# The last stage of a layer kernel: written order for its end, four gate pieces moved into it, other engines for its rows

## The chip, the cores and the metric

The kernel runs on one core of a Trainium2 chip. The metric is the time of one execution on the device in microseconds; lower is better. The core has TensorE (PE, with PEld for its weight loads), VectorE (DVE), ScalarE (ACT), GpSimd (POOL) and SyncE (SP, which issues the DMAs).

## What is computed

One decoder layer on 256 tokens of width 2048, in float32: attention, a mixture of 32 experts of which each token uses two, and an embedding of the layer behind a sigmoid gate; then the final norm.

```python
h = h + mixed @ w_out[i]
m = rms_norm(h, g_moe[i])
h = h + hier_moe(m, ..., w_gate[i], w_up[i], w_down[i])
n = rms_norm(h, g_ple[i])
h = h + jax.nn.sigmoid(n @ w_ple_gate[i]) * (p[i] @ w_ple[i])
return rms_norm(h, g_final)
```

## The kernel before, in words

The tokens are two tiles of 128 rows (`t`), and the 2048 columns are handled in blocks (`BLOCKS`; the last two are 256 wide). The text is about the last stage: while the experts' down products for the later column blocks are still made, the gate product `n @ w_ple_gate` is already summed over the input columns that are finished.

A **unit** of the last two column blocks handles two groups of four experts. `down_rows` makes 32 products into `dn` (L782) and weighs them into `y` on ACT (L790) and DVE (L791); `add_rows` brings them to token rows (L1178) and adds them to `acc` on DVE (L1183). The rows of one unit are added behind the next unit's down products.

A **gate piece** is one 128-row slice of the gate weights by 512 columns. `split_w` cuts it into a high part on ACT and a low part on DVE (L269, L270), two pieces ahead of use, and `gate_part` makes three products for each token tile (L1017 to L1019). There are 56 such pieces, taken from the generator `gate` by `take(steps, n)`, as many for each unit as `PACE` says. Where the last piece of 512 output columns is done, a DVE instruction adds the sum of earlier blocks in PSUM (L1084).

The final 256 input columns come at the very end. Their weights are cut into eight pieces by `last_cuts` (L1041 on ACT; L1042 on DVE, or on POOL for pieces 0, 5 and 6), called **cuts 0 to 7** here. `last_operand` transposes the rows (L1126) and makes `n_hi` on ACT (L1130) and `n_lo` on DVE (L1133). Each of eight **output blocks** (0 to 3 for token tile 0, 4 to 7 for tile 1; 512 columns each) then gets its last two pieces: blocks 0 and 4 need cuts 0 and 1, blocks 3 and 7 need cuts 6 and 7.

For four of the eight blocks, `bank` copies the sum so far into a PSUM bank with ACT (L1145), after a product that sets the bank's state (L1144), and the last products add to it. Then comes `finish`: sigmoid on ACT (L1102), multiplication by the embedding (L1104; blocks 0 to 4 on DVE, 5 to 7 on POOL), addition to `acc` on DVE (L1106), square on ACT with a sum per row (L1108). `norm_rows` makes the factor `r` of a token tile from its four sums (L1091 and L1092 on DVE, a power on POOL, L1093), and `finish_rows` scales each row block by `r` and `g_final` in one DVE instruction (L1119) and issues its output (L1120, on SP's queue). One sigmoid buffer with four places is shared by both token tiles.

What sets the order: the loop over the column blocks stands inside `with tc.manual_schedule():`, which has every engine issue its instructions in the order in which they are written. The part behind that loop, from `last.look(CUT[2])` on, stands outside it; there a scheduler orders each engine's queue, with `RUSH` as a hint of priority for token tile 1. A first sigmoid on a constant (L1149), which makes ACT load the sigmoid's table, also stands outside.

Of the kernel before, what the change touches and what calls it, by code (L numbers as in the profile page):

```python
# [10 lines left out]
F32 = mybir.dt.float32  # L11
# [9 lines left out]
P = 128  # L21
# [15 lines left out]
PLE = 256  # L37
EPS = 1e-6
BIG = 1.0e30
RUSH = ((0, 0, 0, 0, 0), (20, 20, 40, 20, 20))  # L40
CUT = (2, 4, 7, 8)
LAST = (1, 1)
UNITS = (((0, 1), (2, 3), (4, 5), (6, 7)), ((2, 3), (6, 7), (0, 1), (4, 5)))
W4 = 1
ON_V = (0, 1, 2, 3, 4)

EMB = (4, 5)
CUT_G = (0, 5, 6)
LOOK = 2
HURRY = 40  # L50
SECOND = (0, 1)


BLOCKS = ((0, 512), (512, 512), (1024, 512), (1536, 256), (1792, 256))
# [3 lines left out]
PLAN = ((0, (0, 1)), (1, (0, 1)), (2, (0, 1)), (3, (1, 0)))  # L58
WARM = (1, 1)
START = (6, 8)  # L60
PACE = ((0,) + (2,) * 7, (0,) + (2,) * 7, (2, 4, 4, 4), (4, 3, 1, 0))
QA, KA, VA, QB, KB = 0, 1024, 2048, 3072, 4096


# [27 lines left out]
def layer(ctx, tc, T, out):  # L92
# [582 lines left out]
    def take(steps, n):  # L675
        for _ in zip(range(n), steps):
            pass
# [98 lines left out]
        V.tensor_reduce(wrow[:, g : g + 1], tp[:, 0:S], AX.X, ALU.add)  # L776
        V.tensor_scalar(held[:, g, :], tp[:, 0:S], 0.0, None, ALU.is_gt)

    def products(dn, g, wd, q0=0):
        for c in range(2):  # L780
            for q in range(4):
                PE.matmul(  # L782
                    dn[32 * q : 32 * q + 32, :], hid_all[:, g, c, 32 * q : 32 * q + 32], wd[c][:, q0 + q, :],
                    start=(c == 0), stop=(c == 1),
                )

    def weighted(g, dn, y):
# [233 lines left out]
    def cols(cb):  # L1021
        return slice(cb * 512, (cb + 1) * 512)
# [66 lines left out]
    def factor(dst, ss):  # L1089

        V.tensor_reduce(dst, ss, AX.X, ALU.add)  # L1091
        V.tensor_scalar(dst, dst, 1.0 / D, EPS, ALU.mult, ALU.add)  # L1092
        G.tensor_tensor(dst, dst, mhalf, ALU.pow)  # L1093

    def finish(t, cb, ps):
        i = 4 * t + cb
        sg = sgs[:, 512 * (i % 4) : 512 * (i % 4) + 512]
        eb = emb[cb // 2][:, t, 512 * (cb % 2) : 512 * (cb % 2) + 512]
        a = acc[cb][:, t, :]
        E = V if i in ON_V else G  # L1100
        with tc.high_priority(RUSH[t][0]):
            A.activation(sg, ps, AF.Sigmoid, scale=rstd2[:, t : t + 1])  # L1102
        with tc.high_priority(RUSH[t][1]):
            E.tensor_tensor(sg, sg, eb, ALU.mult)  # L1104
        with tc.high_priority(RUSH[t][2]):
            V.tensor_tensor(a, a, sg, ALU.add)  # L1106
        with tc.high_priority(RUSH[t][3]):
            A.activation(sg, a, AF.Square, accum_out=ss4[:, t, cb : cb + 1])  # L1108

    def norm_rows(t):  # L1110
        r = fin.tile([P, 1], F32, name="r", tag="r", bufs=2)
        with tc.high_priority(RUSH[t][4]):
            factor(r, ss4[:, t, :])
        for cb in range(4):
            finish_rows(t, cb, r)

    def finish_rows(t, cb, r):
        o = z[:, t, cols(cb)]
        V.scalar_tensor_tensor(o, acc[cb][:, t, :], r, gfin[:, cols(cb)], ALU.mult, ALU.mult)  # L1119
        nc.sync.dma_start(out[t * P : (t + 1) * P, cols(cb)], o)  # L1120

    def last_operand(t, tp):

# [15 lines left out]

    def bank(t, cb, tag):  # L1140

        ps = psk.tile([P, 512], F32, name="ps", tag=tag, bufs=2 if tag == "sc" else 1)

        PE.matmul(ps, n_hi[0][0:1, 0, 0:P], n_hi[0][0:1, 0:2, :].rearrange("p c t -> p (c t)"), start=True, stop=True)  # L1144
        A.copy(ps, z[:, t, cols(cb)])  # L1145
        return ps


    A.activation(rstd2[:, 0:1], eps, AF.Sigmoid)  # L1149
    mhalf = brt[:, NC + n_groups : NC + n_groups + 1]  # L1150
    G.memset(mhalf, -0.5)
    held_ps = {}
# [1 line left out]
    def down_rows(gs, b, wd, tags, y):  # L1154

        n = BLOCKS[b][1]
        parts = [(j, g, slice(n * j, n * j + n)) for j, g in enumerate(gs)]
        for j, g, part in parts:
            if j < len(tags):
                dn = psk.tile([P, 512], F32, name="dn", tag=tags[j], bufs=1 + (tags[j] == "sc"))  # L1160
            products(dn[:, part], g, wd, 4 * j)
            if len(tags) > 1:
                weighted(g, dn[:, part], y[:, :, part])
        if len(tags) == 1:
            for _, g, part in parts:
                weighted(g, dn[:, part], y[:, :, part])

    def add_rows(gs, b, y):
        n = BLOCKS[b][1]
        ab = block(b)  # L1170
        for t in range(0, NT, 512 // n):
            sc = psk.tile([P, 512], F32, name="sc", tag="sc", bufs=2)
            for i in range(512 // n):
                o = sc[:, n * i : n * i + n]
                rows = slice((t + i) * P, (t + i + 1) * P)
                for j, g in enumerate(gs):
                    for k in range(2):
                        PE.matmul(  # L1178
                            o, held[:, g, rows], y[:, k, n * j : n * j + n],
                            start=(j + k == 0), stop=(j == len(gs) - 1 and k == 1), skip_group_check=True,  # L1180
                        )
            a = ab[:, t : t + 512 // n, :]
            V.tensor_tensor(a, a, sc.rearrange("p (t n) -> p t n", n=n), ALU.add)  # L1183

    with tc.manual_schedule():
# [3 lines left out]
        for b in range(EARLY, len(BLOCKS)):  # L1189
            op = operand(b - 1)  # L1190
            units = [(g,) for g in range(n_groups)] if b < 3 else UNITS[b - 3]
            for u, gs in enumerate(units):
# [7 lines left out]
                if final:  # L1200
                    w_last += [load_gate(b, 0, i)[0] for i in range(W4, 2)]

                    gfin = ring.tile([P, D], "gfin", keep=True)
                    nc.sync.dma_start(gfin, T["g_final"].unsqueeze(0).to_broadcast([P, D]))
                    sgs = ring.tile([P, D], "sg", keep=True)
                    last.look(CUT[0])
                    take(steps, 99)
                    add_rows(*late)
                    banks = {(0, 2): bank(0, 2, "dn")}
                    last.look(CUT[1])  # L1210
                    down_rows(gs, b, wd, ("tp", "sc"), y)
                    add_rows(gs, b, y)
                    break
                down_rows(gs, b, wd, (("tp", "dn")[(len(units) - 1 - u) % 2],), y)
                if late:
# [2 lines left out]
                if u == 0:  # L1218
                    for _ in range(2):
                        take(op, 1)  # L1220
                        take(steps, b > EARLY)
                take(steps, PACE[b - EARLY][u])
                if u == 1:
                    squares(b - 1)
    last.look(CUT[2])

    tp = psk.tile([P, NT, 2, P], F32, name="tpn", tag="tp")
    banks[0, 3] = bank(0, 3, "sc")
    last_operand(0, tp)
    banks[1, 2] = bank(1, 2, "sc")  # L1230
    last.look(CUT[3])
    for t in range(NT):
        for cb in range(4):
            if t == 0:
                last.look(min(8, 2 * cb + LOOK))
            if (t, cb) == SECOND:
                last_operand(1, tp)
            if (t, cb) == LAST:
                banks[1, 3] = bank(1, 3, "tp")
            ps = held_ps[cb][:, t, :] if cb < 2 else banks[t, cb]  # L1240
            for k in range(2):
                gate_part(ps, t, 14 + k, last.ready[2 * cb + k], False, k == 1)
            finish(t, cb, ps)
        norm_rows(t)


NAMES = (
# [41 lines left out]
```

## Time and profile before

| | us |
|---|---|
| median of 3 runs | 900.22 (899.55 to 900.97) |
| the profiled execution | 898.98 |
| its span, first to last instruction | 897.3 |
| PE busy | 818.9 (91%) |
| DVE, ACT, POOL busy | 407.7, 303.7, 73.6 |

A row of a timeline gives start, duration, engine, line, operation, what is written and what is read, and in brackets how long the engine was idle before it and who released it; "x2" merges neighbours of one kind. Times count from the span's start.

### The profile page before, as it was taken

How to read it: one execution, taken by the hardware profiler on the slowest of the kernel's cores; microseconds unless marked ns; L12 is line 12 of the kernel's file. 1: busy time of each engine (PE TensorE's matmuls, PEld its weight loads, DVE VectorE, ACT ScalarE, POOL GpSimd, SP SyncE). 2: the span in 40 equal slices, each digit the busy share in tenths (PEclk: the TensorE clock that was granted, in tenths of full speed). 3: DMA queues.
4: the chain of work that ended last, by engine and by line, in shares of the span. 5: the costliest groups of instructions: out<-in, count | busy, mean ns of one | idle time of the engine just before them, and what ended most of it. 6: DMA issues, size and time to landing. Idle time of an engine off the chain costs nothing. (4 is left out here: it accounts for less than half of the span.)

```text
span 897.3 us, 14941 instructions
## 1 busy us (share of the span) xinstructions
PE 818.9 (91%) x6058; PEld 611.6 (68%) x6058; DVE 407.7 (45%) x857; ACT 303.7 (34%) x624; POOL 73.6 (8%) x93
## 2 busy tenths in 40 slices
PE   9999999999999999999899999998756899989993
PEld 8998987899788886577566656655522455557662
DVE  5778667655565554321212111111200554656666
ACT  5657555644464444100000001010010344334364
POOL 3055133300000001000000000000100000000022
PEclk9999999999999999999999989999978999999997
DMA  9972534445598576499999999999979999999902
GB/s 322 372 214 95 168 115 141 141 142 188 202 415 325 182 278 232 157 415 418 418 420 419 418 418 420 418 419 420 419 304 422 419 420 420 419 420 420 411 5 94
DMA packets 47642, 279.52 MB, mean 312 GB/s; under 512 B 9488, under 2 KB 9808, under 8 KB 16464
## 3 DMA queue, kind: packets, MB, share of 16 engines
q1 hardware_dynamic: 46720, 278.45, 78.2%
q8 instruction: 49, 0.80, 0.4%
q0 software_dynamic: 320, 0.05, 0.2%
q14 instruction: 25, 0.20, 0.1%
q10 hardware_dynamic: 528, 0.01, 0.0%
HBM read 276.39 MB, written 2.10 MB: 310 GB/s over the span
## 5 line engine op out<-in xcount | busy, mean ns | idle before, releaser
L270 DVE TENSOR_TENSOR wl<-w,wh 128x512 fp32r<-128x512 f32 (+1 forms) x208 | 140.4, 682 | 107.1 <-ACT wh L269 102.6
L269 ACT ACTIVATE wh<-w 128x512 fp32r<-128x512 f32 (+1 forms) x208 | 127.1, 615 | 121.1 <-PE ps L289 56.2
L288 PE MATMUL ps<-xn_hi,wh 128*128 128x256 f32 x416 | 118.5, 285 | 0.0
L290 PE MATMUL ps<-xn_hi,wl 128*128 128x256 f32 x416 | 117.9, 283 | 0.2 <-DVE wl L270 0.2
L289 PE MATMUL ps<-xn_lo,wh 128*128 128x256 f32 x416 | 117.7, 283 | 0.0
L694 PE MATMUL px<-gr,h 128*128 128x128 f32 x448 | 105.8, 394 | 10.3 <-DVE gr L684 10.3
L694 PEld LDWEIGHTS px<-gr,h 128*128 128x128 f32 x448 | 100.2, 310 | 21.6 <-DVE gr L684 11.4
L695 DVE TENSOR_TENSOR xg<-px,gmoe 128x512 f32<-128x512 f32 x28 | 19.4, 692 | 142.4 <-PE px L694 142.4
L751 PE MATMUL gu<-wu,xg 128*32 128x256 f32 x1008 | 69.1, 411 | 13.3 <-DMA wu<-in_w_up_dram 11.4
L288 PEld LDWEIGHTS ps<-xn_hi,wh 128*128 128x128 f32 x416 | 78.5, 189 | 1.6 <-issue 1.5
L290 PEld LDWEIGHTS ps<-xn_hi,wl 128*128 128x128 f32 x416 | 78.4, 188 | 1.5 <-issue 0.9
L289 PEld LDWEIGHTS ps<-xn_lo,wh 128*128 128x128 f32 x416 | 78.4, 189 | 0.4 <-issue 0.3
L751 PE MATMUL gu<-wg,xg 128*32 128x256 f32 x1024 | 63.8, 401 | 7.9 <-DVEq L945 6.6
L782 PE MATMUL dn<-wd,hid_all 128*32 128x512 f32 (+1 forms) x640 | 62.6, 513 | 8.2 <-ACT hid_all L763 4.2
L751 PEld LDWEIGHTS gu<-wu,xg 128*32 128x32 f32 x1008 | 34.6, 118 | 43.6 <-DMA wu<-in_w_up_dram 14.3
L791 DVE SCALAR_TENSOR_TENSOR y<-dn,brt,y 128x512 fp32r<-128x512 f32 (+1 forms) x40 | 25.7, 644 | 82.6 <-ACT y L790 82.6
L757 ACT ACTIVATE hs<-gu 128x256 f32<-128x256 f32 x8 | 3.1, 385 | 169.0 <-PE gu L751 169.0
L751 PEld LDWEIGHTS gu<-wg,xg 128*32 128x32 f32 x1024 | 34.0, 116 | 38.0 <-issue 17.0
L522 PE MATMUL ps<-wh,mixed 128*128 128x512 f32 x128 | 51.1, 399 | 0.0
L521 PE MATMUL ps<-wl,mixed 128*128 128x512 f32 x128 | 51.1, 399 | 0.0
L520 PE MATMUL ps<-wh,mixed 128*128 128x512 f32 x128 | 51.0, 398 | 0.0
L790 ACT ACTIVATE y<-dn,brt 128x512 fp32r<-128x512 f32 (+1 forms) x40 | 24.0, 602 | 72.1 <-PE dn L782 64.1
(271 smaller groups left out, 1214.9 us busy)
## 6 DMA issues: line engine op xcount, KB each, us to landing
wg<-in_w_gate_dram SPq DMA_DIRECT2D x64, 1024.0 KB, 18.3
wd<-in_w_down_dram SPq DMA_DIRECT2D x64, 1024.0 KB, 19.9
wu<-in_w_up_dram SPq DMA_DIRECT2D x63, 1024.0 KB, 18.9
w<-in_w_in_dram SPq DMA_DIRECT2D x32, 1024.0 KB, 5.0
w<-in_w_out_dram SPq DMA_DIRECT2D x16, 1024.0 KB, 5.1
wpg<-in_w_ple_gate_dram SPq DMA_DIRECT2D x16, 1024.0 KB, 19.9
h<-in_x_dram SPq DMA_DIRECT2D x8, 256.0 KB, 9.7
w<-in_w_kv_dram SPq DMA_DIRECT2D x4, 512.0 KB, 11.3
```

The lines of the kernel that those rows point to most:

```text
L269: A.activation(wh[:, :n], wv, AF.Copy)
L270: V.tensor_tensor(wl[:, :n], wv, wh[:, :n].bitcast(F32), ALU.subtract)
L288: PE.matmul(o, fh, xn_hi[:, c, :], start=(c == 0 and f % 2 == 0), stop=False, skip_group_check=True)
L289: PE.matmul(o, fh, xn_lo[:, c, :], start=False, stop=False, skip_group_check=True)
L290: PE.matmul(o, fl, xn_hi[:, c, :], start=False, stop=(c == NC - 1), skip_group_check=True)
L520: PE.matmul(o, mh, wh, start=(kc == 8), stop=False, skip_group_check=True)
L521: PE.matmul(o, mh, wl, start=False, stop=False, skip_group_check=True)
L522: PE.matmul(o, ml, wh, start=False, stop=(kc == 7), skip_group_check=True)
L694: PE.matmul(px[:, k, :], h_v[:, t, c + k, :], gr[:, t, :], start=(k == 0 and t == 0), stop=(t == 1), skip_group_check=True)
L751: PE.matmul(gu[32 * q : 32 * q + 32, k, :], xg[:, 8 * i + c, 32 * q : 32 * q + 32], ws[k, i][q][:, c, :], start=(n == 0 and c == 0), stop= ...
L782: PE.matmul(dn[32 * q : 32 * q + 32, :], hid_all[:, g, c, 32 * q : 32 * q + 32], wd[c][:, q0 + q, :], start=(c == 0), stop=(c == 1),)
L791: V.scalar_tensor_tensor(y[:, 1], dn, w, y[:, 0].bitcast(F32), ALU.mult, ALU.subtract)
```

## The change

The tail moves into the manual region, so that its order is the written one, and its loop is written anew. In turn i come the cut for a later piece, the products of output block i, its sigmoid and multiplication, then the square of block i - 1; the rows of tile 0 are written behind block 4. Four of the 56 gate pieces are left for the last unit and the tail (`PACE`). The last unit makes its down products before the rows of the unit before it, in one bank. `bank` has no setting product any more, and `products` starts a bank only once. Each of the eight sigmoids has its own place. Blocks 2 and 5 are multiplied on POOL, the others on DVE. All four row blocks of tile 0, and the last one of tile 1, are scaled by ACT and multiplied by `g_final` on POOL; three of tile 1 stay on DVE. The first sigmoid on a constant moves into the first unit of the last column block.

```diff
@@ -37,18 +37,14 @@
...
-RUSH = ((0, 0, 0, 0, 0), (20, 20, 40, 20, 20))
-CUT = (2, 4, 7, 8)
-LAST = (1, 1)
...
-ON_V = (0, 1, 2, 3, 4)
+ON_G = (2, 5)
...
-LOOK = 2
...
-SECOND = (0, 1)
@@ -58,7 +54,7 @@
...
 START = (6, 8)
-PACE = ((0,) + (2,) * 7, (0,) + (2,) * 7, (2, 4, 4, 4), (4, 3, 1, 0))
+PACE = ((0,) + (2,) * 7, (0,) + (2,) * 7, (2, 4, 4, 4), (3, 1, 0))
 QA, KA, VA, QB, KB = 0, 1024, 2048, 3072, 4096
@@ -776,12 +772,12 @@
...
-    def products(dn, g, wd, q0=0):
+    def products(dn, g, wd, q0=0, first=True):
         for c in range(2):
...
                     dn[32 * q : 32 * q + 32, :], hid_all[:, g, c, 32 * q : 32 * q + 32], wd[c][:, q0 + q, :],
-                    start=(c == 0), stop=(c == 1),
+                    start=(c == 0 and first), stop=(c == 1), skip_group_check=True,
                 )
@@ -1093,31 +1089,31 @@
...
     def finish(t, cb, ps):
         i = 4 * t + cb
-        sg = sgs[:, 512 * (i % 4) : 512 * (i % 4) + 512]
-        eb = emb[cb // 2][:, t, 512 * (cb % 2) : 512 * (cb % 2) + 512]
+        sg = sgs[i // 4][:, 512 * (i % 4) : 512 * (i % 4) + 512]
         a = acc[cb][:, t, :]
-        E = V if i in ON_V else G
-        with tc.high_priority(RUSH[t][0]):
-            A.activation(sg, ps, AF.Sigmoid, scale=rstd2[:, t : t + 1])
-        with tc.high_priority(RUSH[t][1]):
-            E.tensor_tensor(sg, sg, eb, ALU.mult)
-        with tc.high_priority(RUSH[t][2]):
+        A.activation(sg, ps, AF.Sigmoid, scale=rstd2[:, t : t + 1])
+        (G if i in ON_G else V).tensor_tensor(sg, sg, emb[cb // 2][:, t, 512 * (cb % 2) : 512 * (cb % 2) + 512], ALU.mult)
+        if i not in ON_G:
             V.tensor_tensor(a, a, sg, ALU.add)
-        with tc.high_priority(RUSH[t][3]):
-            A.activation(sg, a, AF.Square, accum_out=ss4[:, t, cb : cb + 1])
+        yield
+        if i in ON_G:
+            V.tensor_tensor(a, a, sg, ALU.add)
+        A.activation(sg, a, AF.Square, accum_out=ss4[:, t, cb : cb + 1])
+        yield
...
         r = fin.tile([P, 1], F32, name="r", tag="r", bufs=2)
-        with tc.high_priority(RUSH[t][4]):
-            factor(r, ss4[:, t, :])
+        factor(r, ss4[:, t, :])
         for cb in range(4):
-            finish_rows(t, cb, r)
-    def finish_rows(t, cb, r):
-        o = z[:, t, cols(cb)]
-        V.scalar_tensor_tensor(o, acc[cb][:, t, :], r, gfin[:, cols(cb)], ALU.mult, ALU.mult)
-        nc.sync.dma_start(out[t * P : (t + 1) * P, cols(cb)], o)
+            o, a = z[:, t, cols(cb)], acc[cb][:, t, :]
+            if t and cb < 3:
+                V.scalar_tensor_tensor(o, a, r, gfin[:, cols(cb)], ALU.mult, ALU.mult)
+            else:
+                A.activation(o, a, AF.Copy, scale=r)
+                G.tensor_tensor(o, o, gfin[:, cols(cb)], ALU.mult)
+            nc.sync.dma_start(out[t * P : (t + 1) * P, cols(cb)], o)
@@ -1139,14 +1135,11 @@
...
         ps = psk.tile([P, 512], F32, name="ps", tag=tag, bufs=2 if tag == "sc" else 1)
-        PE.matmul(ps, n_hi[0][0:1, 0, 0:P], n_hi[0][0:1, 0:2, :].rearrange("p c t -> p (c t)"), start=True, stop=True)
         A.copy(ps, z[:, t, cols(cb)])
...
-    A.activation(rstd2[:, 0:1], eps, AF.Sigmoid)
     mhalf = brt[:, NC + n_groups : NC + n_groups + 1]
@@ -1158,7 +1151,7 @@
...
                 dn = psk.tile([P, 512], F32, name="dn", tag=tags[j], bufs=1 + (tags[j] == "sc"))
-            products(dn[:, part], g, wd, 4 * j)
+            products(dn[:, part], g, wd, 4 * j, j < len(tags))
             if len(tags) > 1:
@@ -1177,7 +1170,7 @@
...
                             o, held[:, g, rows], y[:, k, n * j : n * j + n],
-                            start=(j + k == 0), stop=(j == len(gs) - 1 and k == 1), skip_group_check=True,
+                            start=(i + j + k == 0), stop=(j == len(gs) - 1 and k == 1), skip_group_check=True,
                         )
@@ -1202,14 +1195,15 @@
...
                     nc.sync.dma_start(gfin, T["g_final"].unsqueeze(0).to_broadcast([P, D]))
-                    sgs = ring.tile([P, D], "sg", keep=True)
-                    last.look(CUT[0])
-                    take(steps, 99)
+                    sgs = [ring.tile([P, D], "sg", keep=True) for _ in range(2)]
+                    down_rows(gs, b, wd, ("tp",), y)
                     add_rows(*late)
+                    last.look(2)
+                    take(steps, 2)
+                    last.look(4)
+                    add_rows(gs, b, y)
                     banks = {(0, 2): bank(0, 2, "dn")}
-                    last.look(CUT[1])
-                    down_rows(gs, b, wd, ("tp", "sc"), y)
-                    add_rows(gs, b, y)
+                    take(steps, 1)
                     break
@@ -1219,29 +1213,38 @@
...
                         take(steps, b > EARLY)
+                if (b, u) == (4, 0):
+                    A.activation(rstd2[:, 0:1], eps, AF.Sigmoid)
                 take(steps, PACE[b - EARLY][u])
...
                     squares(b - 1)
-    last.look(CUT[2])
-    tp = psk.tile([P, NT, 2, P], F32, name="tpn", tag="tp")
-    banks[0, 3] = bank(0, 3, "sc")
-    last_operand(0, tp)
-    banks[1, 2] = bank(1, 2, "sc")
-    last.look(CUT[3])
-    for t in range(NT):
-        for cb in range(4):
-            if t == 0:
-                last.look(min(8, 2 * cb + LOOK))
-            if (t, cb) == SECOND:
+        tp = psk.tile([P, NT, 2, P], F32, name="tpn", tag="tp")
+        last_operand(0, tp)
+        take(steps, 99)
+        banks[0, 3] = bank(0, 3, "sc")
+        ends = None
+        for i in range(8):
+            t, cb = divmod(i, 4)
+            last.look(min(8, i + 5))
+            if i == 0:
                 last_operand(1, tp)
-            if (t, cb) == LAST:
-                banks[1, 3] = bank(1, 3, "tp")
+                banks[1, 2] = bank(1, 2, "sc")
+            if i == 5:
+                banks[1, 3] = bank(1, 3, "dn")
             ps = held_ps[cb][:, t, :] if cb < 2 else banks[t, cb]
...
                 gate_part(ps, t, 14 + k, last.ready[2 * cb + k], False, k == 1)
-            finish(t, cb, ps)
-        norm_rows(t)
+            nxt = finish(t, cb, ps)
+            take(nxt, 1)
+            if ends:
+                take(ends, 1)
+            ends = nxt
+            if i == 4:
+                norm_rows(0)
+        take(ends, 1)
+        norm_rows(1)
...
 NAMES = (
```

## Rows read from the trace of the kernel before

**Rows 1.** The page's busy tenths, 40 slices of 22.4 us.

```profile
DMA  9972534445598576499999999999979999999902
```

**Rows 2.** Instructions of tile wd from 820 us: durations in ns min/median/max, starts; landing.

```profile
L83 SPq DMA_DIRECT2D wd<-in_w_down_dram x3: 327/328/333, 821.2 to 828.6; - x3
...
DMA to landing us min/median/max: 18.1/20.1/20.2
```

**Rows 3.** Stretches: us, busy PE, PEld, DVE, ACT, POOL, PEclk (granted clock), DMA.

```profile
869.00:873.00 4.00, 4.00 (x12) 3.14 (x13) 1.31 (x6) 2.94 (x7) 1.13 (x2) 0.57 0.01 2
873.00:882.00 9.00, 9.00 (x38) 6.63 (x36) 6.89 (x13) 7.37 (x19) 1.50 (x2) 1.00 0.00 0
882.00:893.00 11.00, 0.08 (x1) 0.00 (x0) 9.48 (x15) 3.32 (x10) 3.50 (x4) 0.70 0.32 123
```

**Rows 4.** Timeline of PE: down products of the last two units, first transposes.

```profile
856.16 1.93 PE L782 MATMUL dn<-wd,hid_all 128*32 128x256 f32 x32
...
861.53 0.50 PE L1144 MATMUL ps<-n_hi 1*128 1x512 f32 x1
861.96 1.93 PE L782 MATMUL dn<-wd,hid_all 128*32 128x256 f32 x32
...
867.02 0.50 PE L1126 MATMUL tpn<-ident,acc 128*128 128x128 f32 x2 [0.35 <-DVE acc L1183]
```

**Rows 5.** Timeline of DVE and ACT, 859 to 864 us.

```profile
859.70 0.48 DVE L791 SCALAR_TENSOR_TENSOR y<-dn,brt,y 128x256 fp32r<-128x256 f32 x1 [0.54 <-ACT y L790]
...
862.06 0.59 ACT L1145 COPY ps<-h 128x512 f32<-128x512 f32 x1 [1.36 <-PE ps L1144]
862.59 1.15 ACT L1041 ACTIVATE w_hi<-wpg 128x512 fp32r<-128x512 f32 x2
```

**Rows 6.** Groups from 860 us: busy us, mean ns, idle before and its releaser.

```profile
L1041 ACT ACTIVATE w_hi<-wpg 128x512 fp32r<-128x512 f32 x8 | 4.6, 623 | 0.0
L1104 POOL TENSOR_TENSOR sg<-sg,emb 128x512 f32<-128x512 f32 x3 | 3.9, 1314 | 9.8 <-ACT sg L1102 9.8
L1104 DVE TENSOR_TENSOR sg<-sg,emb 128x512 f32<-128x512 f32 x5 | 3.3, 687 | 3.3 <-ACT sg L1102 3.3
L1133 DVE SCALAR_TENSOR_TENSOR n_lo<-tpn,brt,n_hi 128x128 fp32r<-128x128 f32 x4 | 1.3, 341 | 0.0
L1130 ACT ACTIVATE n_hi<-tpn,brt 128x128 fp32r<-128x128 f32 x4 | 1.2, 364 | 0.3 <-PE tpn L1126 0.3
L1084 DVE TENSOR_TENSOR ps<-ps,h 128x1024 f32<-128x1024 f32 x1 | 1.2, 1230 | 0.0
```

**Rows 7.** Timeline of POOL and DVE, 878 to 888 us.

```profile
878.13 1.29 DVE L1104 TENSOR_TENSOR sg<-sg,emb 128x512 f32<-128x512 f32 x2 [0.82 <-ACT sg L1102]
...
880.50 2.53 POOL L1104 TENSOR_TENSOR sg<-sg,emb 128x512 f32<-128x512 f32 x2 [9.26 <-ACT sg L1102]
...
881.83 1.74 DVE L1106 TENSOR_TENSOR acc<-acc,sg 128x512 f32<-128x512 f32 x1 [1.20 <-POOL sg L1104]
...
885.59 1.38 POOL L1104 TENSOR_TENSOR sg<-sg,emb 128x512 f32<-128x512 f32 x1 [0.53 <-ACT sg L1102]
...
885.76 1.75 DVE L1119 SCALAR_TENSOR_TENSOR h<-acc,r,gfin 128x512 f32<-128x512 f32 x1
```

**Rows 8.** Timeline of ACT, POOL and DVE, from 871 us.

```profile
871.08 1.28 ACT L1102 ACT_TABLE_LOAD   x1 [1.05 <-issue]
...
874.53 0.69 ACT L1102 ACTIVATE sg<-ps,rstd 128x512 f32<-128x512 f32 x1 [0.38 <-PE ps L1019]
875.12 0.62 ACT L1108 ACTIVATE sg<-acc 128x512 f32<-128x512 f32 x1
...
884.51 0.55 POOL L1093 TENSOR_TENSOR r<-r,brt 128x1 f32<-128x1 f32 x1 [1.48 <-DVE r L1092]
...
884.84 0.67 ACT L1102 ACTIVATE sg<-ps,rstd 128x512 f32<-128x512 f32 x1
...
890.57 2.74 DVE L1119 SCALAR_TENSOR_TENSOR h<-acc,r,gfin 128x512 f32<-128x512 f32 x4 [0.66 <-POOL r L1093]
```

## The prediction

> **What bounds the kernel now.** I read the busy slices first [rows 1]: the DMA engines are full up to the slice that ends at 852 us and idle after it. So nothing behind 853 us can wait for a load, and the last two loads of w_down land by 828.6 + 20.2 = 848.8 us [rows 2]. Then the stretches of the end [rows 3]: TensorE has work without a hole from 873 to 882 us; from 882 to 893 us it does nothing, and DVE is busy 9.48 of 11 us. The end is a chain of small instructions, and the order in each engine's queue decides it. Third, the order itself. Inside the manual region queues hold the written order: at 862.06 ACT waits 1.36 us for the bank's product although the cuts written behind that copy [rows 5] had their weights since the DMAs ended, 9 us before [rows 1]. The tail stands outside the region, and there the square of block 0 runs at 875.12, behind the sigmoids of blocks 1 and 2 [rows 8]: the scheduler had reordered it. The change puts the tail into the region, so I take its queues in written order.
>
> **The sum, part by part.** The profiled execution took 898.98 us for a span of 897.3; the median of the runs is 900.22, so 1.24 is to be added to what I get against the profile.
>
> *Four gate pieces later.* A product takes 9.00/38 = 0.237 us [rows 3], a piece of six 1.4 us. One piece fewer runs in the first unit of the last block, two fewer in the second, one fewer in the third, so the last unit's down product, 861.96 before [rows 4], starts near 855.0: 5.6 us of pieces, and 1.4 because the previous unit's rows and the first setting product (0.5) no longer stand before it. No load moves: the last gate load is issued in the first unit in both. The extra sigmoid buffer pushes the cut weights into slots last read by the second and third unit's down products, which are done by 854. Cost and gain here are nothing, covered by DMAs that ended at 853 [rows 1].
>
> *Up to the first transposes.* Here DVE counts, not PE. From the end of a down product to its last y is 860.18 - 858.09 = 2.1 us [rows 4, 5], so y is there at 859.0. DVE then has an addition, the cut of piece 1 (kept out by POOL's cut 0 until 860.4, see the port below), two cuts for the late pieces, the sum on the bank of 1.23, two more cuts, and the addition that ends the block: 0.6 + 1.4 + 1.2 + 1.1 + 1.2 + 0.7 = 6.2 us, a DVE instruction taking 0.69 alone [rows 6] and 0.6 behind another, two in 1.29 [rows 7]. The transposes start at 865.2, against 867.02 [rows 4]: **1.8 us gained**. PE has two of the late pieces in front of the last rows and one behind, and still waits 1.7 us.
>
> *From there to the norm of the first token tile.* Transposes, two n_hi (0.36), two n_lo (0.34) [rows 6] and the second transposes take 2.4 us, so block 0 runs 867.6 to 869.0. The sigmoid table load of 1.28 [rows 8] is gone from here (it lies in the first unit of the last block, where cuts are made two pieces, 2.8 us, ahead; without that cover it would cost its 1.3). But cuts 5, 6 and 7 are now written behind sigmoids and squares. ACT: sigmoid 0 at 869.3 (0.69), cut 5 at 869.9, sigmoid 1 at 870.7, square 0, cut 6 (an ACT instruction is 0.62 to 0.69 [rows 6, 8]). Square 0 needs the addition of block 0, and that is kept out by POOL's cut 5 (870.6 to 871.9) and ends at 872.4; so cut 6 is at 873.1, POOL's half of it 873.8 to 875.1, and block 3, which TensorE could begin at 872.3, has its first lower half at 875.1. POOL's multiplication of block 2 is next to 876.3, DVE's cut 7 behind it to 876.9; block 3 ends at 877.4. Sigmoid 3 877.7, multiplication, addition, addition of block 2 to 880.3, square 2, sigmoid 4, square 3 to 882.2; then reduce, scale, power (0.55 on POOL [rows 8]) with block 4's two DVE instructions before them: the factor r of tile 0 is there at **883.8**, against 885.06 (884.51 + 0.55 [rows 8]). A PE wait of some 3 us eats most of what the pieces gave; 1.3 us stays.
>
> *From r to the last row.* Now POOL's queue has, in this order, r, four row products of tile 0, the multiplication of block 5. ACT scales the first row (0.62, the price of a cut on ACT [rows 6], to which it is nearest), POOL starts at 884.5 and needs 4 x 1.27 = 5.1 us: a POOL product is 1.31 alone and 2.53 for two [rows 6, 7]. Block 5's sigmoid is ready at 887.1 and waits in that queue; with DVE's multiplication of block 6 let in between, its product ends at 891.3. Queued behind it: addition 5 (after addition 6) to 892.5, square 5, and on ACT, behind square 5, sigmoid 7, at **893.1**, where it began at 884.84 before [rows 8]. Then multiplication and addition to 895.1, square to 895.9, reduce, scale, power to 896.9, three rows on DVE and the fourth on ACT and POOL, which shut each other out once: last row at 900.1. Before it is 890.57 + 2.74 = 893.31 [rows 8]: **6.8 us later**. Two rows now end within 0.6 us and their outputs are issued one behind the other, 0.4 more. Sum **+7.2 us**.
>
> The same addition along before's own queues, from 861.5 on, puts its last row at 894.1 where the trace has 893.31: 0.8 too late. I take that off: +6.4, so 906.6 against the median.
>
> **The port of DVE and POOL.** At 881.83 a DVE addition takes 1.74 instead of 0.69, ending 0.54 after POOL's second product (880.50 + 2.53), and at 885.76 a row takes 1.75, 0.54 after POOL's end [rows 7]. So an instruction that is kept out loses the other's remaining time, less about 0.14 that overlaps. The sum uses this at eight places. The Trainium skill (SBUF — State Buffer, section SBUF: two separate sides) has the shared pair as an exclusive lock, the loser blocked for the whole instruction, and its next section measured a start 115 ns behind the end. The trace agrees that it blocks, and differs on the hand-over. By the page's figure eight hand-overs at 0.14 + 0.115 more make some 2.0 us, an estimate, and the time would be 908.6.
>
> **Bounds.** If nothing were kept out, the same chains give r at 881.5 and the last row at 895.7: +2.4, and +0.4 for the outputs, less 0.8, is 902.2. Above: hand-overs without overlap are 8 x 0.14 = 1.1 us. The clock: TensorE's granted clock was 0.57 from 869 to 873 us [rows 3], most of the stretch at its lower level, 1.2 GHz, after it had waited for the last rows and for DVE's addition up to 867.02 [rows 4]; waits like those at 863, 871 and 873 us can bring it again, which in these chains adds 0.4 to 0.8. Together 908.5, and 0.3 either way for what no row shows: ACT's scaled copy of a row, taken as a cut's 0.62, lies between a bank's copy, 0.59 [rows 5], and a sigmoid, 0.69 [rows 8], and there are four. The removed setting products (0.5 each) free PE where it waits anyway: nothing, except for block 7's bank, which no longer waits on PE but on ACT behind four row copies (886.0); sigmoid 7 is later than that for another reason, so this too is covered, and would cost at most 4 us in its own chain.
>
> **Rivals.**
> *The ports do not collide* (the products meet other instructions than I set beside them): 902.2 as above. For it: the meetings depend on tenths. Against: POOL has 5 us of row products in one piece, DVE must work in them. Chance 0.15.
> *The cuts come in time and the ports do not collide*: block 3 then ends at 873.2, r comes 4 us earlier, and what POOL has queued still sets the last row near 894: about 900.5, no change. Against: cut 7 is written after square 1 on ACT, by hand. Chance 0.07.
> *Faster: sigmoid 7 does not queue behind square 5.* Place: ACT's queue. If queues took what is ready (the order not kept, so that the change does not do what it says), PE would end at 867.6 + 8 x 1.4 = 878.8 instead of 882.1 and the tail after it would be as before: -3.2, 897.0. It decides where sigmoid 7 starts: before 884.8 the change gains, after it it loses. For it: the pieces and the table load do free 1.8 us by the transposes. Against: ACT's wait at 862.06 [rows 5]. Chance 0.11.
>
> **Numbers.** The forecast, late cuts and block 5 behind the rows, has 0.67. About 1.8 us (0.2%) is what a measurement of this kernel can tell from no change. Predicted 906.6; the range is 901.8 to 909.5: the low end takes in the case without collisions, the high end the bounds above. Faster 0.11 (the third rival), same 0.07 (the second), slower 0.82.
>
> **What would show it.** Right: the last unit's down product near 855, transposes near 865, holes in PE at 871 to 877, POOL with four products in a row from about 884.5 and the fifth of block 5 behind them, sigmoid 7 near 893 and behind a square, no table load in the tail. Wrong: sigmoid 7 before 885, POOL's row products running beside full-speed DVE instructions, or r before 879.

## The result, and the profile of the changed kernel

The changed kernel takes 908.65 us in the median of four runs (907.32 to 910.13), the kernel before 899.88 on the same chip: a ratio of 1.0096, 95% interval 1.0077 to 1.0114. The profiled execution took 910.13 us for a span of 908.1. Up to the last column block nothing that matters differs, but its first down product starts at 836.93 in this trace and at 835.21 in that of before. These 1.72 us are the execution's own (in the runs below, whose code is the same up to there, the start lies between 833.4 and 836.5), so they are taken off wherever a place below is compared with the prediction.

The first view is TensorE's timeline: start, duration, instruction, and in brackets how long the engine was idle and who released it.

```profile
856.70 1.93 PE L778 MATMUL dn<-wd,hid_all 128*32 128x256 f32 x32
...
866.85 0.51 PE L1122 MATMUL tpn<-ident,acc 128*128 128x128 f32 x2 [1.89 <-DVE acc L1176]
867.11 0.51 PE L1013 MATMUL ps<-wh,n_hi 128*128 128x512 f32 x1
...
869.25 0.77 PE L1013 MATMUL ps<-w_hi,n_hi 128*128 128x512 f32 x1
...
874.68 0.51 PE L1014 MATMUL ps<-w_lo,n_hi 128*128 128x512 f32 x1 [0.41 <-POOL w_lo L1038]
...
876.50 0.49 PE L1013 MATMUL ps<-w_hi,n_hi 128*128 128x512 f32 x1 [1.09 <-ACT w_hi L1037]
877.85 0.50 PE L1014 MATMUL ps<-w_lo,n_hi 128*128 128x512 f32 x1 [0.86 <-POOL w_lo L1038]
...
879.65 0.80 PE L1014 MATMUL ps<-w_lo,n_hi 128*128 128x512 f32 x1 [0.61 <-DVE w_lo L1038]
...
890.43 0.50 PE L1013 MATMUL ps<-w_hi,n_hi 128*128 128x512 f32 x1 [3.33 <-ACT ps L1140]
```

The last unit's down product and the transposes, 861.96 and 867.02 before [rows 4], stand 5.3 and 0.2 us earlier in spite of the 1.72. Between 874 and 880 us TensorE stops four times, once in block 2 and three times in block 3, each time for a cut of the last weights (`w_hi`, `w_lo`): ACT made them behind sigmoids and squares, and two of the lower halves (`w_lo`) came from POOL. Block 7 starts only at 890.43, released by the copy to its bank.

The stretches (us, busy PE, PEld, DVE, ACT, POOL, granted clock, DMA) show what the waits also cost, against [rows 3].

```profile
867.00:873.00 6.00, 6.00 (x22) 4.72 (x23) 3.61 (x11) 4.52 (x13) 1.13 (x2) 0.72 0.00 0
...
880.00:888.00 8.00, 7.11 (x20) 5.23 (x19) 3.59 (x7) 3.25 (x8) 0.55 (x1) 0.67 0.00 0
888.00:893.00 5.00, 1.66 (x6) 1.05 (x6) 0.78 (x1) 4.18 (x9) 4.86 (x4) 1.00 0.32 125
893.00:904.00 11.00, 0.00 (x0) 0.00 (x0) 7.66 (x10) 3.35 (x8) 4.05 (x4) 0.61 0.22 86
```

After the idle 1.89 us the granted clock is 0.72, after the four stops it is 0.67: part of each stretch is at the lower level, 1.2 GHz. From 888 to 893 us DVE is busy 0.78 of 5 us while POOL is full. The next three fences are its timelines of POOL, of DVE and of ACT; they say with what.

```profile
873.34 1.29 POOL L1038 TENSOR_TENSOR w_lo<-wpg,w_hi 128x512 fp32r<-128x512 f32 x1 [0.90 <-ACT w_hi L1037]
...
877.76 1.28 POOL L1097 TENSOR_TENSOR sg<-sg,emb 128x512 f32<-128x512 f32 x1
886.76 0.55 POOL L1089 TENSOR_TENSOR r<-r,brt 128x1 f32<-128x1 f32 x1 [7.72 <-DVE r L1088]
888.14 4.95 POOL L1115 TENSOR_TENSOR h<-h,gfin 128x512 f32<-128x512 f32 x4 [0.83 <-ACT h L1114]
893.04 1.72 POOL L1097 TENSOR_TENSOR sg<-sg,emb 128x512 f32<-128x512 f32 x1
```
```profile
873.50 1.67 DVE L1099 TENSOR_TENSOR acc<-acc,sg 128x512 f32<-128x512 f32 x1
...
878.19 1.40 DVE L1038 TENSOR_TENSOR w_lo<-wpg,w_hi 128x512 fp32r<-128x512 f32 x1 [1.69 <-ACT w_hi L1037]
...
892.22 1.43 DVE L1097 TENSOR_TENSOR sg<-sg,emb 128x512 f32<-128x512 f32 x1 [5.54 <-ACT sg L1096]
893.68 1.63 DVE L1099 TENSOR_TENSOR acc<-acc,sg 128x512 f32<-128x512 f32 x1
895.24 0.68 DVE L1102 TENSOR_TENSOR acc<-acc,sg 128x512 f32<-128x512 f32 x1
...
900.56 3.08 DVE L1112 SCALAR_TENSOR_TENSOR h<-acc,r,gfin 128x512 f32<-128x512 f32 x3 [0.66 <-POOL r L1089]
```
```profile
872.05 0.69 ACT L1096 ACTIVATE sg<-ps,rstd 128x512 f32<-128x512 f32 x1 [0.90 <-issue]
...
880.91 0.69 ACT L1096 ACTIVATE sg<-ps,rstd 128x512 f32<-128x512 f32 x1 [2.75 <-PE ps L1015]
...
887.34 2.56 ACT L1114 ACTIVATE h<-acc,r 128x512 f32<-128x512 f32 x4 [1.75 <-POOL r L1089]
889.81 0.57 ACT L1140 COPY ps<-h 128x512 f32<-128x512 f32 x1
890.32 0.68 ACT L1096 ACTIVATE sg<-ps,rstd 128x512 f32<-128x512 f32 x1
...
895.95 0.63 ACT L1103 ACTIVATE sg<-acc 128x512 f32<-128x512 f32 x1 [3.76 <-DVE acc L1102]
...
896.58 0.67 ACT L1096 ACTIVATE sg<-ps,rstd 128x512 f32<-128x512 f32 x1
```

Read them as one chain: r of tile 0 at 887.31 (886.76 + 0.55); four row products on POOL to 893.09; block 5's product behind them to 894.76; its addition at 895.24; its square at 895.95; and behind that square, on ACT, sigmoid 7 at 896.58, where before it began at 884.84 [rows 8]. The last row ends at 903.64 (900.56 + 3.08).

### The profile page after: what moved, and what is told of

Its sections match the earlier page's. It is cut to its first block, busy times and chain, and to the rows that moved or that the text cites. A ratio compares the mean times of both kernels' runs of the same rounds, so it can differ in the third digit from the quotient of the medians.

```text
span 908.1 us, 14932 instructions
## 1 busy us (share of the span) xinstructions
PE 822.7 (91%) x6054; PEld 613.1 (68%) x6054; DVE 407.6 (45%) x853; ACT 304.0 (33%) x627; POOL 79.3 (9%) x97
## 5 line engine op out<-in xcount | busy, mean ns | idle before, releaser
L747 PE MATMUL gu<-wu,xg 128*32 128x256 f32 x1008 | 72.1, 424 | 11.8 <-DMA wu<-in_w_up_dram 9.5
```

The lines of the kernel that those rows point to most:

```text
L747: PE.matmul(gu[32 * q : 32 * q + 32, k, :], xg[:, 8 * i + c, 32 * q : 32 * q + 32], ws[k, i][q][:, c, :], start=(n == 0 and c == 0), stop= ...
```

## The experiments

Every run is given as its ratio to the kernel before, with the 95% interval, and as that ratio's microseconds on 899.9; the changed kernel is at +8.6. The table holds places in the profiled executions in microseconds, each counted from the first down product of the last column block in the same trace (the timeline's start less that product's start).

```
kernel                     transposes  sigmoid 0  r, tile 0  PE's end  sigmoid 7  last row
before                        31.8       37.2       49.9       46.9      49.6       58.1
changed                       29.9       35.1       50.4       55.2      59.7       66.7
cuts early                    31.0       36.2       46.7       52.7      56.0       63.0
rows of tile 0 on DVE         29.9       33.8       48.6       49.3      55.0       62.1
no POOL products              29.8       33.7       45.6       46.7      50.4       57.1
scheduler's order             29.9       33.3       44.5       42.5      47.6       56.1
cuts early, rows mid          31.1       36.1       50.2       47.1      52.7       60.6
norm first                    31.0       36.0       46.5       47.0      52.4       60.3
last row taken apart          29.8       34.7       43.3       44.4      48.1       54.1
the same, scheduler's order   29.8       34.8       43.4       42.7      43.2       53.1
```

The first four runs each undo one part. Three theories stood against each other: the queue (what is written behind a late instruction waits with it), the port (DVE and POOL shut each other out), the clock (TensorE at 1.2 GHz).

**Cuts early.** All eight cuts written in front of the transposes.

```diff
                     banks = {(0, 2): bank(0, 2, "dn")}
                     take(steps, 1)
+                    last.look(8)
```

> The changed kernel with one line more: all eight cuts are written before the tail, so that cuts 4 to 7 no longer stand behind sigmoids and squares. Queue theory (late cuts delay the factor r of tile 0; block 5 behind the row products delays sigmoid 7 the rest): r 2.8 us earlier, 2.8 us faster than the changed kernel's 908.7, about 905.9; sigmoid 7 still behind square 5 and the row products. Clock theory (the loss is TensorE at 1.2 GHz after the holes in its work, 4.8 us in the changed kernel's trace): no holes, so up to 4.8 us faster, about 903.9. Port theory (the loss is DVE and POOL keeping each other out, about 6 us in the trace, wherever the cuts stand): the same collisions, about 908, no difference.

Measured 1.0061 (1.0042 to 1.0079), +5.5: 3.1 less. The four stops for cuts are gone and r is 3.7 us earlier although the transposes are 1.1 later. The lower clock behind those stops is gone with them (the products of 870 to 879 us start 0.23 apart), so the saving holds both. The queue theory had said 2.8; the port theory's 908 lies outside the interval. The clock theory's bound, 903.9 or 1.0044, lies just inside it, so this run alone does not exclude it; behind the transposes the lower clock is still there (granted 0.57 from 866 to 869 us).

**Block 5 on DVE.**

```diff
-ON_G = (2, 5)
+ON_G = (2,)
```

> The changed kernel with block 5 multiplied on DVE, so that it does not wait in POOL's queue behind the four row products. Queue theory: r unchanged, sigmoid 7 some 1.8 us earlier (DVE's multiplication still meets POOL's rows), about 906.8. Clock theory: nothing changes, TensorE is done by then: 908.7. Port theory: three of the eight collisions go, worth 1.4 to 2 us: 907.

Measured 1.0068 (1.0050 to 1.0086), +6.1: 2.5 less, against the queue theory's 1.8, the port's 1.4 to 2 and the clock's none. The interval leaves out the clock theory's 908.7 (1.0098); queue and port are not told apart.

**Rows of tile 0 on DVE.**

```diff
-            if t and cb < 3:
+            if cb < 3 or t == 0:
```

> The changed kernel with the four row blocks of token tile 0 in one DVE instruction each, as in the kernel before; POOL keeps block 5 but nothing stands before it, and ACT has no row copies. Queue theory: r unchanged, sigmoid 7 about 3 us earlier, last row 3 us earlier: 905.6. Clock theory: 908.7, no change. Port theory: four long POOL products less, two or three collisions less: 906 to 907.

Measured 1.0060 (1.0041 to 1.0078), +5.4: 3.2 less, against 3.0 of the queue theory. ACT's four row copies go with POOL's products here. Block 5's product behind POOL's rows costs 2.5 to 3.2 us, its collisions included, whichever of the two leaves POOL. The intervals of these first three runs meet the changed kernel's (1.0077 to 1.0114) at the edge or overlap it: each saving by itself is known to about 2 us either way. The clock has a side of its own here. This is the stretch behind the transposes with block 5 on DVE (columns as above):

```profile
863.90:869.90 6.00, 5.90 (x26) 4.27 (x26) 4.79 (x12) 5.29 (x14) 2.10 (x3) 1.00 0.01 1
```

TensorE had waited 1.89 us for the transposes there too, and so it had with the rows on DVE; in both executions the clock then stayed at 1.00, where it is 0.72 in the changed kernel's. That is the 1.3 us by which sigmoid 0 differs in the table, and it is no part of the edits, which change nothing before it. The ratios are over all executions; how the clock fell in those without a profile is not known.

**No POOL products.** Cuts, multiplications and rows all on DVE; the order stays as written.

```diff
-ON_G = (2, 5)
+ON_G = ()
-CUT_G = (0, 5, 6)
+CUT_G = ()
...
-            if t and cb < 3:
+            if True:
```

> The changed kernel, its written order kept, with no wide POOL instruction in the last stage: all low cuts, all multiplications by the embedding and all row blocks on DVE (POOL keeps the powers on one column). Queue theory with the port: r 3.4 us earlier, sigmoid 7 some 8 us earlier, 9 us faster than the changed kernel: about 899.6, level with the kernel before at 899.9 or a little under it. Port theory alone: the 6 us of collisions go: 902.7. Clock theory: at most a part of 4.8 us: 904 or more. If the written order itself were the loss, it would stay near 908.

Measured 1.0004 (0.9992 to 1.0016): 8.2 less, the time of before. Queue and port together had said 899.6, the ratio gives 900.3; the port alone and the clock fall, and so does the written order by itself (near 908). POOL's ten large products, in this order, carry nearly the whole loss.

**Scheduler's order.** POOL keeps all ten; only the tail leaves the manual region.

```diff
-        tp = psk.tile([P, NT, 2, P], F32, name="tpn", tag="tp")
-        last_operand(0, tp)
+    tp = psk.tile([P, NT, 2, P], F32, name="tpn", tag="tp")
+    last_operand(0, tp)
...
```

> The changed kernel with the tail's lines moved back out of the manual region, so that the scheduler orders them; every instruction and every engine stays. Theory A (written order and POOL's work together): the cuts move ahead of the transposes, worth about 3 us by the run that did that alone, and block 5's product ahead of the rows of tile 0; POOL still has 13 products of 1.26 us with DVE kept out beside them, so the time is about 903.5 (902.5 to 904.7) where the kernel before takes 899.2. Theory B (the written order alone is the cost): 897, the time of the prediction's third rival, with sigmoid 7 before 885 on the span. Theory C (POOL's work alone, the order does not matter): as the changed kernel, 907.8.

Measured 0.9989 (0.9976 to 1.0002), -1.0: near theory B's time, 897 of 899.2, which lies at the interval's edge. Theory A's time fell, and its count was wrong as well (ten products, not 13). But "the written order alone" is not the cost either, because without POOL's products that order takes the time of before too (1.0004). The loss comes of the two together: the same work on the same engines, in another order, takes the time of before. TensorE's timeline, the stretch behind the transposes, POOL's timeline and DVE's show how.

```profile
865.17 0.50 PE L1122 MATMUL tpn<-ident,acc 128*128 128x128 f32 x2 [0.50 <-DVE acc L1176]
866.12 0.50 PE L1013 MATMUL ps<-w_hi,n_hi 128*128 128x512 f32 x1 [0.46 <-ACT n_hi L1126]
```
```profile
866.00:869.00 3.00, 2.88 (x13) 2.42 (x14) 2.76 (x10) 2.27 (x8) 1.78 (x2) 1.00 0.01 5
```
```profile
876.12 1.30 POOL L1097 TENSOR_TENSOR sg<-sg,emb 128x512 f32<-128x512 f32 x1 [2.71 <-ACT sg L1096]
878.79 0.93 POOL L1089 TENSOR_TENSOR r<-r,brt 128x1 f32<-128x1 f32 x1 [1.36 <-DVE r L1088]
880.55 5.38 POOL L1115 TENSOR_TENSOR h<-h,gfin 128x512 f32<-128x512 f32 x4 [0.83 <-ACT h L1114]
```
```profile
883.52 1.28 DVE L1097 TENSOR_TENSOR sg<-sg,emb 128x512 f32<-128x512 f32 x1 [3.49 <-ACT sg L1096]
```

All four late gate pieces now run in front of the transposes, so the 1.89 us of waiting shrink to 0.50 and block 0 follows 0.46 behind the transposes; in the written order the fourth piece stands behind the transposes (867.11 above), in front of block 0. The clock stays at 1.00, TensorE's eight blocks run without a stop to 877.75, block 5's product (876.12) is ahead of the rows, and the rows run mostly in 3.49 us in which DVE had nothing to do.

**Rows late.** Does moving the rows behind everything do the same?

```diff
-            if i == 4:
+            if i == 7:
                 norm_rows(0)
```

> The changed kernel with the norm and rows of tile 0 written behind block 7 instead of block 4, still on ACT and POOL. Queue theory (block 5's product behind four row products is what sets the end): sigmoid 7 starts some 5 us earlier on the span (about 891) and takes the end along: 903 to 905. Sum theory (POOL's 5 us of row products have to be done before the last tile's own row, wherever they stand): sigmoid 7 is 5 us earlier all the same, but r of tile 0 and its rows are later and the end stays: 907 to 908.5.

Measured 1.0087 (1.0068 to 1.0105), +7.8: no gain that stands out of the intervals. For this place the sum theory holds; that the rows cost as much wherever they stand does not follow, as the scheduler's order above shows. Counted from the second unit's down product (848.71 here, 849.29 in the changed kernel; the first unit ran longer in this execution, at a granted clock of 0.88 where it was 1.00), sigmoid 7 is 6.0 us earlier, but the queue has only moved, as the timelines of ACT and then POOL show:

```profile
890.02 0.67 ACT L1096 ACTIVATE sg<-ps,rstd 128x512 f32<-128x512 f32 x1
...
893.13 2.56 ACT L1114 ACTIVATE h<-acc,r 128x512 f32<-128x512 f32 x4 [1.83 <-POOL r L1089]
895.59 0.61 ACT L1103 ACTIVATE sg<-acc 128x512 f32<-128x512 f32 x1
```
```profile
893.92 4.93 POOL L1115 TENSOR_TENSOR h<-h,gfin 128x512 f32<-128x512 f32 x4 [0.83 <-ACT h L1114]
898.80 0.55 POOL L1089 TENSOR_TENSOR r<-r,brt 128x1 f32<-128x1 f32 x1
```

Block 7's square now waits behind four row copies on ACT, and the power of tile 1 behind four row products on POOL.

**Cuts early, rows mid.** The written order with two moves: the cuts of the first run, and the rows behind block 6.

```diff
+                    last.look(8)
...
-            if i == 4:
+            if i == 6:
                 norm_rows(0)
```

> The changed kernel, order still written by hand, with two moves: all eight cuts written ahead of the transposes, and the norm and rows of tile 0 written behind block 6 instead of block 4, so that block 5's product stands ahead of the row products on POOL. POOL keeps its work. Theory A (these two lines are what the written order costs): about the time of the run in the scheduler's order, 897 to 898.5. Theory B (they are a part; other places, such as the last bank's copy behind the rows on ACT, cost as well): 900.5 to 903, near the 902 that the changed kernel's chains give with both moves. Theory C (moving the rows is worth nothing, as in the run that put them last): as the run with early cuts alone, 904 to 905.

Measured 1.0047 (1.0031 to 1.0063), +4.2. Theory A falls: two lines aren't what the written order costs. B and C can't be told apart by this interval; the trace is 2.4 us ahead of the run with early cuts at the last row. Two things remain in its rows (TensorE's timeline, the stretch behind it, DVE's timeline):

```profile
866.47 0.70 PE L1122 MATMUL tpn<-ident,acc 128*128 128x128 f32 x2 [2.96 <-DVE acc L1176]
```
```profile
866.00:869.00 3.00, 2.53 (x7) 2.14 (x8) 2.84 (x7) 1.51 (x5) 0.95 (x1) 0.58 0.00 0
```
```profile
884.63 0.15 DVE L1087 TENSOR_REDUCE r<-ss4f 128x1 f32<-128x4 f32 x1
```

TensorE waits 2.96 us for the transposes and then has a granted clock of 0.58; and the reduction for r stands on DVE behind the additions of blocks 6 and 5, though its last square was done at 880.4.

**Bank too.** The copy to block 7's bank behind block 2, beside the moves of the last run.

```diff
-            if i == 5:
+            if i == 3:
                 banks[1, 3] = bank(1, 3, "dn")
```

> As the run before it, and the copy to the bank of block 7 is written behind block 2's sigmoid instead of in front of block 5. If the bank's copy held TensorE and sigmoid 7 up: 1 us or more below that run, TensorE done 1 us earlier. If sigmoid 7 waits for squares and POOL's products anyway: within 0.8 us of that run.

Measured 1.0047 (1.0030 to 1.0064), the same to the fourth digit. TensorE ends 1.4 us earlier and sigmoid 7 is 0.4 later (53.0 on the table's scale): the bank held up only TensorE.

**Norm first.** As cuts early, rows mid, with `norm_rows` in two: the norm of tile 0 is back behind block 4, its rows stay behind block 6, but now in front of block 5's addition and square, where they stood behind them.

```diff
...
             take(nxt, 1)
+            if i == 6:
+                rows(0, r0)
             if ends:
                 take(ends, 1)
             ends = nxt
-            if i == 6:
-                norm_rows(0)
+            if i == 4:
+                r0 = norm(0)
...
```

> As the run with early cuts and the rows behind block 6, but the norm of tile 0 is written behind block 4 again and its rows in front of block 5's square: so the reduction does not stand behind block 5's and block 6's additions on DVE, where it was ready about 4 us before it ran, and block 5's product is still ahead of the rows on POOL. If that place in DVE's queue is one of the remaining costs of the written order: r about 4 us earlier on the span, sigmoid 7 about 2 us earlier, and 1.5 to 2.5 us less than that run (1.0047 of before), 1.0020 to 1.0030. If the earlier start of TensorE and its clock are all that is left between that run and the scheduler's order: r earlier, but the end within 0.8 us of that run, 1.0038 to 1.0056.

Measured 1.0031 (1.0018 to 1.0044): the interval holds both expectations. The trace is for the second: r is 3.6 us earlier, sigmoid 7 0.3, the last row 0.4. Two places moved at once, so what the norm's place is worth alone stays open. POOL's rows now stand beside DVE's additions of blocks 6 and 5, and both engines are slower for it (timelines of POOL and DVE):

```profile
881.20 6.25 POOL L1118 TENSOR_TENSOR h<-h,gfin 128x512 f32<-128x512 f32 x4
```
```profile
881.80 1.64 DVE L1099 TENSOR_TENSOR acc<-acc,sg 128x512 f32<-128x512 f32 x1
883.36 1.75 DVE L1102 TENSOR_TENSOR acc<-acc,sg 128x512 f32<-128x512 f32 x1
```

**Three runs for a faster kernel.** The first has no POOL products and early cuts.

```diff
-ON_G = (2, 5)
-CUT_G = (0, 5, 6)
+ON_G = ()
+CUT_G = ()
...
-            if t and cb < 3:
+            if True:
...
+                    last.look(8)
```

> No large product on POOL, and all eight cuts ahead of the transposes. Theory A (both causes, but DVE is nearly full once it has everything): the cuts take three times 0.69 us of DVE out of the stretch behind the transposes and fill a wait of 1.25 us in front of them, 1.7 us less than with the products off POOL alone: about 897.3, some 0.2 per cent faster than before. If the two gains simply add (3.1 and 8.2): 896.0 or less. If the cuts mattered only because POOL made them: 898.8 to 899.3, no change.

Measured 0.9980 (0.9967 to 0.9993), -1.8: theory A, a small gain over before. The second also takes the very last row apart:

```diff
+        if t:
+            V.tensor_tensor(z[:, t, cols(3)], acc[3][:, t, :], gfin[:, cols(3)], ALU.mult)
         factor(r, ss4[:, t, :])
...
+                A.activation(o, o, AF.Copy, scale=r)
```

> As the run with no POOL products and early cuts, and the last row of tile 1 is taken apart: DVE multiplies it by g_final while it waits for the last square, ACT scales it by r (0.72 us) beside DVE's three other rows. If DVE's last row (0.67 us) sets the end: 0.6 to 0.7 us less than that run, about 896.6. If the added DVE product (0.69 us) delays the factor r: no gain, 897.3.

Measured 0.9968 (0.9955 to 0.9982), -2.9. Expected was 0.7 below the run before it; the measured 1.1 has intervals that overlap, but DVE's last group is three rows in place of four. The third is this kernel with its tail in the scheduler's order:

```diff
-        tp = psk.tile([P, NT, 2, P], F32, name="tpn", tag="tp")
+    tp = psk.tile([P, NT, 2, P], F32, name="tpn", tag="tp")
...
```

> The kernel without POOL products, with early cuts and the last row taken apart, its tail in the scheduler's order. If the written order costs something without POOL too (a sigmoid behind a square, a cut behind a sigmoid): 1 to 2 us below the written one, 894.5 to 895.5 where the kernel before takes 898.5. If DVE, full behind the transposes, sets the end: no difference, 896 to 897.

Measured 0.9954 (0.9939 to 0.9968), -4.1, the fastest here. The end of its timelines of DVE and ACT:

```profile
882.91 0.69 DVE L1109 TENSOR_TENSOR h<-acc,gfin 128x512 f32<-128x512 f32 x1
...
884.69 2.08 DVE L1114 SCALAR_TENSOR_TENSOR h<-acc,r,gfin 128x512 f32<-128x512 f32 x3 [0.66 <-POOL r L1089]
```
```profile
884.69 0.72 ACT L1116 ACTIVATE h<-h,r 128x512 f32<-128x512 f32 x1 [1.04 <-POOL r L1089]
```

The product with g_final runs while DVE waits for the last square, and ACT scales that row beside DVE's three. The order gains 1.3 us here by the ratios, with intervals that overlap; in the traces the last row is 1.0 earlier. Against the scheduler's order with POOL's products (0.9989), this kernel is 3.1 us faster, and these intervals do not overlap; the last row taken apart gave 1.1 of it. So in that order too POOL's products seem to cost something, by an estimate up to 2 us; early cuts are the other difference of the two kernels.

## Why the prediction was right, and where its sizes were off

**Direction and mechanism: shown.** Late cuts stop TensorE in blocks 2 and 3, and block 5's product waits on POOL behind four rows, and sigmoid 7 behind block 5's square. The runs that undo the one (3.1 us) or the other (2.5 and 3.2) give back what such steps should, each to about 2 us either way; that POOL's products in this order carry the loss stands on the 8.2 us without them and the 9.6 in the scheduler's order.

**Up to the transposes: right.** Down product at 856.70 - 1.72 = 854.98 (forecast 855.0), transposes at 865.13 (865.2).

**To r of tile 0: 1.8 us short.** Block 0 starts at 867.5 as forecast (867.6), but its sigmoid starts at 872.05 - 1.72 = 870.3 where 869.3 was said, and sigmoid 3 at 879.2 where 877.7 was; r is there at 885.6, not 883.8. The term that was mis-sized is the clock: the prediction kept it out of the sum, as a bound of 0.4 to 0.8 us. TensorE's products start 0.43 us apart from 868.5 to 871.5 and from 880.2 to 884.9, against 0.23 at 2.4 GHz. That makes 1.0 us by sigmoid 0 and 1.5 by sigmoid 3; the last 0.3 lies behind sigmoid 3, in the chain of ACT and DVE. In other executions the first of the two stretches is at the full clock: there r is at 884.3 (block 5 on DVE) and 883.8 (rows on DVE) on the scale of before, with the same instructions up to r. So most of the 1.8 us belongs to this execution; how the clock fell in the other three is not known.

**From r to the last row: right.** Four rows take 4.95 us (forecast 5.1). Sigmoid 7 starts 9.3 us behind r (forecast 9.3), the last row ends 7.1 behind that (7.0). ACT's row copies take 0.71 each where 0.62 was taken, but only the first of them is on the path. The outputs end 4.46 us behind the last row, against 897.3 - 893.31 = 3.99 before: 0.47 (0.4).

**The 0.8 us taken off** for the lateness of the same addition along before's queues should have stayed in. With the 1.8 us above that is 2.6 us; the span less 1.72 is 906.4, the prediction's sum gives 897.3 + 6.4 = 903.7, so 2.7 were missing in this execution. By the ratio, 8.6 against 6.4, it is 2.2. The result lies near the top of the bounds that the prediction added up (908.5, and 0.3 either way); the stated 909.5 is wider than that sum.

**The port: right.** POOL's cut ends at 874.63 and DVE's addition 0.54 later, at 875.17; at 879.04 and 879.59 it is 0.55. Alone such an instruction takes 0.69, so 0.14 or 0.15 overlap, as the prediction had it. The Trainium skill (SBUF — State Buffer, section SBUF: two separate sides) has the pair as an exclusive lock: the traces agree that it blocks. The 115 ns of its section "A bandwidth-pool intuition that's wrong (but worth ruling out)" were measured on a DMA whose descriptors waited for a DVE copy; carried over to this pair, an estimate, the end would be 0.69 + 0.115 = 0.81 behind. The traces show 0.54 and 0.55, and they decide. That the 908.6 worked out from that figure comes to within 0.1 of the measured median is luck: what was missing was the clock and the 0.8 us, not the hand-overs.

**The third rival** named its condition well: with the tail in the scheduler's order the change gives the loss back. Its 897.0 was too good: the measured ratio makes 899.2 of 900.22. TensorE did end at 877.75, even before the 878.8 that were said, but sigmoid 7 stands behind four row copies on ACT and is 2.0 us ahead of before in the table, not 3.2.

**One step said too much.** Sigmoid 7 was made the point that decides. Rows late moved it by 6 us and the end hardly at all: the 5 us of row products then stood ahead of tile 1's power instead. By the traces, what counts is whether POOL's rows meet a gap of DVE's and have nothing urgent behind them; no run tests that by itself.

**What stays open.** How the rest between norm first and the scheduler's order (0.4% of ratio) splits between the fourth gate piece's place, the clock, and POOL's rows beside DVE. The fourth piece alone was not moved, so its part is argued from the rows, not shown.

## What to carry to other kernels

When a tail is written by hand, follow every queue past each moved instruction, and ask what is urgent behind it on that queue: ten POOL products cost 8 us in one order and, by the estimate above, 2 at most in another. A slower engine is a place for work only where the faster one has a gap at that time. At the very end, look for what can be multiplied before the last factor is known.

## What was not expected of the hardware

The one-column power on POOL takes 0.55 us alone and 0.93 beside a DVE instruction (878.79 in the scheduler's order). ACT's copy of a 128x512 row with a factor per row takes 0.71 us, a plain copy to a bank 0.57. TensorE's granted clock was 0.58 in the stretch behind an idle 2.96 us and 1.00 behind waits of 0.50 and 0.46. Behind the same wait of 1.89 us (1.90 with the rows late) it was 0.72 in the changed kernel's execution and in that with the rows late, and 1.00 in two others. The length of the wait alone does not tell: block 7 of the changed kernel ran at 1.00 (888 to 893 us) behind an idle 3.33 us.
